# Layers of a transformer on one core: two hand-ordered stages get their orders from a search over priorities

## The chip, the cores and the metric

The kernel runs on one core of one Trainium2 chip. The metric is the device time of one launch in microseconds (us). A core has a matrix engine (PE, with its weight loads shown as PEld), a vector engine (DVE), an activation engine (ACT), a general engine (POOL) and a sync engine (SP) that issues most loads. Each engine takes its instructions in the order in which the program lists them, and waits for what the others have to deliver.

## The reference

The reference runs two layers of a first block on 256 latent and 256 context tokens of width 1024, and then one layer of a second block on the latent tokens. All is float32. Only the mixers of the first block's two layers matter here.

```python
# layer 0, half of the mixer: a delta rule over time, 8 heads of 64, forwards and backwards,
# first over the context, then over the latent tokens
def step(state, inp):
    r_t, w_t, k_t, v_t, kk_t, a_t = inp
    sa = jnp.einsum('bhvk,bhk->bhv', state, -kk_t)
    state = (state * w_t[:, :, None, :] + sa[..., None] * (kk_t * a_t)[:, :, None, :]
             + v_t[..., None] * k_t[:, :, None, :])
    return state, jnp.einsum('bhvk,bhk->bhv', state, r_t)
...
out_lat = jnp.concatenate([a_lat, b_lat], axis=-1) @ w_out
# layer 1's mixer: neighbourhood attention (8 heads) beside global attention (8 heads, 2 of keys),
# both with the context's keys and values, then w_out
```

After each mixer come a normalised residual, a squared-ReLU MLP (1024 to 4096 to 1024) and another residual.

## The kernel before, in words

Weights are split into a rounded part and a rest (`whi` on ACT, `wlo` on DVE, lines 608 and 609), activations likewise, and each product is made of three passes on PE. Loads of 512 KB (`raw`) come over SP's queue into a ring of three buffers.

Most of the kernel is put in order by the compiler's own scheduler. Two stages are not: between `flow.open` and `flow.close` every call on an engine is only recorded, with what it reads and writes, and `close` then issues all of them in an order of its own for PE, DVE, ACT and POOL. In the profile all of their instructions have line 501, where `close` issues them. SP's issues stay with the compiler's scheduler.

The first such stage is the delta rule. For each of 4 tiles (two heads each) `kappa(t)` normalises keys (with an rsqrt on POOL, `rsn`). For each of 16 blocks (tile, direction, context or latent) `rwkv_par` makes the decays (`sg`, `cs`, `E`, `kr`, `bk`), the masked products `GK`, `Gt`, then five rounds of a triangular inverse (`Tp` on DVE, `pq` on PE, `Qm` on DVE, `px` or `psT` on PE, `Sp` on ACT), and the matrices `KX`, `QM`. `rwkv_rec` carries the state over four chunks (`yp` on PE, `S` on DVE and ACT). `rwkv_out` normalises a finished tile (`yN`, `sqy`, `moA`). Beside these chains stand pieces that nothing in the stage waits for soon: 12 calls of `ada_chunk` (modulation weights of later stages, `psT<-raw,sT`, PE tiles of 128x32), three projections of the delta rule's own inputs for tile 3, and the first part of the output projection (`proj0`). PSUM banks are shared out in rings: banks 0 and 1 for the preparation, 2 for `pq`, 3, 4 and 5 one for each block in flight, 6 for the recurrence, 7 for `ada_chunk`, `gates_out` and `rwkv_out` in program order.

The second stage is layer 1's mixer: projections, rsqrts for the normalised heads (`rk`, `rq` on POOL), the bias sums `bC`, 8 calls of `attn4`, and the output projection.

The order comes from `order`. `links` finds for each recorded operation what it must wait for, and its `way`, the longest chain of durations from it to the end. `order` then plays the stage through: at each step, of the operations of the engine that can start first, those that could start within 100 ns of the earliest are compared, and the one with the longest way is taken. PE has a bonus of 2000 ns of way for staying in the same tile shape, and a price of 100 ns for changing it. The durations are formulas, for instance (line 343 for DVE, 347 for POOL; `both` is 2 in the delta rule, 1.05 in the mixer):

```python
o.dur = 150 + 2.8 * n if op.endswith("scan") else 150 + 1.03 * n if psum else 170 + (self.both if ins > 1 else ...) * n
...
o.dur = 1650 if k.get("op") == OP.pow else 200 + (1.3 if ... else 2.4 if self.both > 1.5 or op != "tensor_scalar" else 3.2) * n
```

The time at which the last engine is free in this play is the tally, `self.span`.

Of the kernel before, what the change touches and what calls it, by code (L numbers as in the profile page):

```python
# [3 lines left out]

# [262 lines left out]
class _Flow:  # L267
# [156 lines left out]
                p = ops[j]  # L424
                p.way = max(getattr(p, "way", 0), o.way + (p.tail if p.key != o.key else 0))

    def order(self, slack=100, stay=2000):
        self.links()
        ops = self.ops
        nxt, left = [[] for _ in ops], [len(o.pre) for o in ops]  # L430
        for i, o in enumerate(ops):
            o.new = [r for r in {x[0] for x in o.w + o.r if isinstance(x[0], _Root)} if r.place is None and r.heir is None]
            for j in o.pre:
                nxt[j].append(i)
        ready, free, mode, grid = {i for i, n in enumerate(left) if not n}, {}, None, {}
        idle, out = {}, []
        for r in self.roots:
            if r.place is None and r.heir is None:
                r.todo = len(r.ops)
                idle.update({x: 0 for x in r.places})  # L440
        while ready:
            start = {}
            for i in ready:
                o = ops[i]
                st = max(o.at, free.get(o.key, 0))
                if o.key == "T":
                    st = max([st] + [grid.get(c, 0) for c in o.parts[0][0]]) if o.mode == mode else \
                        max([st] + [x + 100 for x in grid.values()])
                for r in o.new:
                    if r.place is None:  # L450
                        st = max(st, min((idle[x] for x in r.places if x in idle), default=1e12))
                start[i] = st
            best = {}
            for i in ready:
                best[ops[i].key] = min(best.get(ops[i].key, 1e12), start[i])
            key = min(best, key=best.get)
            assert best[key] < 1e12
            i = max((i for i in ready if ops[i].key == key and start[i] <= best[key] + slack),
                    key=lambda i: (ops[i].way + (stay if key == "T" and ops[i].mode == mode else 0), -i))
            ready.discard(i)  # L460
            o, st = ops[i], start[i]
            for r in o.new:
                if r.place is None:
                    r.place = min((x for x in r.places if x in idle), key=lambda x: idle[x])
                    del idle[r.place]
            end = st + o.dur
            if o.key == "T":
                mode, at = o.mode, st
                for cells, n, recs in o.parts:

                    at = max([at] + [grid.get(c, 0) for c in cells])
                    for c in cells:
                        grid[c] = at + n
                    end = at + n
                    at += 7 * recs
                free["T"] = at
            else:
                free[o.key] = end
            out.append((st, i))
            for r in o.new:  # L480
                r.todo -= 1
                r.till = max(getattr(r, "till", 0), end + o.tail)
                if not r.todo:
                    idle[r.place] = r.till
            for j in nxt[i]:
                left[j] -= 1
                ops[j].at = max(ops[j].at, end + (o.tail if ops[j].key != o.key else 0))
                if not left[j]:
                    ready.add(j)
        self.span = max(free.values())  # L490
        return [i for _, i in sorted(out)]

    def close(self, engines):
        self.on = False
# [12 lines left out]
def body(ctx: ExitStack, tc: tile.TileContext, A, out, dbg=None):  # L507
# [982 lines left out]
    def proj_rows(W, x_of, tiles, done, order=(0, 1, 2, 3), between=None):  # L1490


        ps = {i: B_O0("pso") for i in tiles}
        for n_, q in enumerate(order):
            wh, wl = wchunk(W, q * 256, 2, 0, 512)
            for i in tiles:
                for k in range(2):
                    mmX(ps[i], *x_of(2 * q + k, i), wh[:, k, :], wl[:, k, :], n_ + k == 0, n_ == 3 and k == 1)
        if between is not None:
            between()  # L1500
        ws = wrows(W, 0, 8, 512)
        for i in tiles:
            p_ = B_O1("pso")
            for k in range(8):
                mmX(p_, *x_of(k, i), *ws[k], k == 0, k == 7)
            done(i, [ps[i], p_])
# [682 lines left out]
```

## Time and profile before

| | us |
|---|---|
| median of 3 runs | 1804.53 |
| lowest and highest | 1802.65, 1807.39 |
| the profiled execution | 1798.13 |
| its span, first to last instruction | 1796.2 |

The profile shows one execution. Busy times are those of an engine's instructions; a PE matmul's end is modelled. The granted clock is a mean over a stretch, 1.00 for TensorE's full speed. In lists of waits each line says which engine waited, for which engine's result, how long in total, how often, and the longest.

### The profile page before, as it was taken

Reading aid. Unit: us, or ns where it says so; the run is one execution under the profiler, and the core shown is the slowest. Engines: PE = TensorE matmul, PEld = TensorE weight load, DVE = VectorE, ACT = ScalarE, POOL = GpSimd, SP = SyncE. Lnnn points to the kernel's source line nnn. Section 1 sums busy time; section 2 is a strip of 40 time slices with the busy share of each in tenths; the row PEclk is TensorE's granted clock in tenths of the full one; section 3 lists DMA queues with packets and bytes.
Section 4 is the critical chain, followed back from the end, with each engine's and each line's share of the span. In section 5 each row is a group of like instructions: output and inputs, shape, how many; then the busy total and the mean of one; then the engine's idle time right before and its main releaser. Section 6 shows DMA issues by size and latency. Waiting matters only on the chain.

```text
span 1796.2 us, 33992 instructions
## 1 busy us (share of the span) xinstructions
PE 1715.3 (95%) x13601; PEld 1440.3 (80%) x13601; DVE 1082.0 (60%) x1965; ACT 884.1 (49%) x1703; POOL 447.2 (25%) x512
## 2 busy tenths in 40 slices
PE   6999899999898999999998999899989999999998
PEld 4777677767577888888887887799978889989997
DVE  3577577766656334444464775655566686568776
ACT  4555245544345554443443655545555554446553
POOL 1120344542413343333332213311120211110000
PEclk9999899999899999999998999999999999999999
DMA  9322141222264454444423322465547436655553
GB/s 311 108 59 60 37 140 51 96 74 95 72 198 142 131 169 147 141 141 141 141 82 87 89 71 71 132 197 187 188 152 226 129 93 174 190 156 187 177 183 121
DMA packets 185407, 240.08 MB, mean 134 GB/s; under 512 B 8961, under 2 KB 127889, under 8 KB 185121
## 3 DMA queue, kind: packets, MB, share of 16 engines
q1 hardware_dynamic: 183056, 229.68, 41.1%
q0 software_dynamic: 1904, 7.70, 1.3%
q8 instruction: 107, 1.75, 0.4%
q10 hardware_dynamic: 288, 0.52, 0.1%
q14 instruction: 52, 0.42, 0.1%
HBM read 236.83 MB, written 1.05 MB: 132 GB/s over the span
## 4 chain that ended last, share of the span: by engine, by line
PE 86%; DVE 5%; DMA 3%; ACT 2%; POOL 2%; issue 2%; SPq 0%; POOLq 0%; DVEq 0%; ACTq 0%
PE psT L623 9%; PE psT L625 9%; PE psT L624 9%; PE psT L501 9%; PE pf L628 6%; PE pf L629 6%; PE pf L630 6%; PE px L501 3%; PE ssp L501 2%; PE psr L501 2%; PE psU L623 2%; PE psU L625 2%; PE psU L624 2%; PE pq L501 2%; PE yp L501 2%; PE psS L501 2%
## 5 line engine op out<-in xcount | busy, mean ns | idle before, releaser
L609 DVE TENSOR_TENSOR wlo<-raw,whi 128x1024 fp32r<-128x1024 f32 x291 | 358.4, 1239 | 245.7 <-ACT whi L608 242.6
L608 ACT ACTIVATE whi<-raw 128x1024 fp32r<-128x1024 f32 x291 | 306.4, 1056 | 235.2 <-PE psT L624 121.6
L623 PE MATMUL psT<-uh,whi 128*128 128x256 f32 (+1 forms) x1032 | 332.4, 327 | 2.8 <-ACT uh L909 1.2
L624 PE MATMUL psT<-ul,whi 128*128 128x256 f32 (+1 forms) x1032 | 330.7, 321 | 0.0
L625 PE MATMUL psT<-uh,wlo 128*128 128x256 f32 (+1 forms) x1032 | 328.4, 321 | 0.0
L623 PEld LDWEIGHTS psT<-uh,whi 128*128 128x128 f32 x1032 | 193.3, 189 | 21.6 <-ACT uh L909 1.7
L624 PEld LDWEIGHTS psT<-ul,whi 128*128 128x128 f32 x1032 | 193.4, 188 | 17.9 <-issue 1.1
L625 PEld LDWEIGHTS psT<-uh,wlo 128*128 128x128 f32 x1032 | 193.5, 188 | 16.1 <-issue 0.3
L630 PE MATMUL pf<-whi,hlo 128*128 128x512 f32 x472 | 182.4, 390 | 0.0
L629 PE MATMUL pf<-wlo,hh 128*128 128x512 f32 x472 | 182.3, 390 | 0.0
L628 PE MATMUL pf<-whi,hh 128*128 128x512 f32 x472 | 181.9, 392 | 0.0
L1512 POOL TENSOR_TENSOR ffr<-ffr 128x512 f32<-128x512 f32 (+1 forms) x64 | 64.3, 1004 | 283.2 <-ACT hh L1511 251.7
L630 PEld LDWEIGHTS pf<-whi,hlo 128*128 128x128 f32 x472 | 88.6, 188 | 18.8 <-issue 0.2
L629 PEld LDWEIGHTS pf<-wlo,hh 128*128 128x128 f32 x472 | 88.6, 188 | 17.5
L628 PEld LDWEIGHTS pf<-whi,hh 128*128 128x128 f32 x472 | 88.5, 188 | 17.5
L623 PE MATMUL psU<-uh,whi 128*128 128x256 f32 x352 | 99.0, 282 | 1.0 <-DVE cv L2101 1.0
L624 PE MATMUL psU<-ul,whi 128*128 128x256 f32 x352 | 98.5, 280 | 0.0
L625 PE MATMUL psU<-uh,wlo 128*128 128x256 f32 x352 | 98.5, 280 | 0.0
L1513 DVE TENSOR_TENSOR hlo<-ffr,hh 128x512 fp32r<-128x512 f32 (+1 forms) x64 | 47.6, 743 | 76.9 <-POOL ffr L1512 76.9
L717 POOL TENSOR_TENSOR adac<-adac,wadc 128x512 f32<-128x512 f32 x56 | 76.2, 1361 | 64.0 <-ACT wadc L715 50.4
L715 ACT ACTIVATE wadc<-wadc,sT 128x512 f32<-128x512 f32 x56 | 40.5, 724 | 98.3 <-DMA wadc<-in_w_ada_dram 96.8
L623 PEld LDWEIGHTS psU<-uh,whi 128*128 128x128 f32 x352 | 66.6, 189 | 1.9 <-ACT whi L608 0.9
(775 smaller groups left out, 3603.1 us busy)
## 6 DMA issues: line engine op xcount, KB each, us to landing
raw<-in_w_ff_dram SPq DMA_DIRECT2D x128, 512.0 KB, 4.5
raw<-in_w_in_dram SPq DMA_DIRECT2D x50, 512.0 KB, 4.4
raw<-in_w_ada_dram SPq DMA_DIRECT2D x48, 512.0 KB, 4.7
raw<-in_w_ffn_up_dram SPq DMA_DIRECT2D x44, 512.0 KB, 4.8
wadc<-in_w_ada_dram SPq DMA_DIRECT2D x64, 256.0 KB, 2.9
raw<-in_w_out_dram SPq DMA_DIRECT2D x24, 512.0 KB, 3.7
raw<-in_w_ffn_down_dram SPq DMA_DIRECT2D x22, 512.0 KB, 4.5
raw<-in_w_in_even_dram SPq DMA_DIRECT2D x21, 512.0 KB, 4.2
```

The lines of the kernel that those rows point to most:

```text
L501: b = f(*map(real, a), **{n: real(x) for n, x in k.items()})
L608: S.activation(hi[:, :tot], raw[:, :tot], AF.Copy)
L609: V.tensor_tensor(lo[:, :tot], raw[:, :tot], R(hi[:, :tot]), op=OP.subtract)
L623: T.matmul(p_, wh, xh, start=first, stop=False)
L624: T.matmul(p_, wh, xl, start=False, stop=False)
L625: T.matmul(p_, wl, xh, start=False, stop=last)
L628: T.matmul(p_, xh, wh, start=first, stop=False)
L629: T.matmul(p_, xh, wl, start=False, stop=False)
L630: T.matmul(p_, xl, wh, start=False, stop=last)
L717: G.tensor_tensor(acc, acc, w, op=OP.add)
L1512: G.tensor_tensor(r_, r_, r_, op=OP.mult)
L1513: V.tensor_tensor(hl_, r_, R(hh), op=OP.subtract)
```

## The change

`order` now calls the old procedure, renamed `greedy`, once with the ways from `links`, and then 400 times with changed ways. For each trial it takes 1, 3 or 10 places in the list of operations, and adds to the ways of 1, 1, 5, 20 or 80 operations from there a number between -15000 and 15000 ns. A trial whose tally is not longer than the best so far becomes the base of the next. The best schedule's order, and its places for those PSUM tiles that have a choice, are issued. The random numbers are seeded, so the program is the same each time. `close` is as before, and so are the recorded operations, their durations and what they wait for.

```diff
-    def order(self, slack=100, stay=2000):
+    def order(self, rounds=400):
+
         self.links()
-        ops = self.ops
+        rng, way = random.Random(1), [o.way for o in self.ops]
+        best = self.greedy(way)
+        for _ in range(rounds):
+            w, n = list(way), len(way)
+            for _ in range(rng.choice((1, 3, 10))):
+                k, m, d = rng.randrange(n), rng.choice((1, 1, 5, 20, 80)), rng.uniform(-15e3, 15e3)
+                for x in range(k, min(n, k + m)):
+                    w[x] += d
+            new = self.greedy(w)
+            if new[0] <= best[0]:
+                best, way = new, w
+        self.span, seq, places = best
+        for r, x in places:
+            r.place = x
+        return seq
+
+    def greedy(self, way, slack=100, stay=2000):
+        ops, taken = self.ops, []
+        for r in self.roots:
+            if r.places is not None:
+                r.place, r.till = None, 0
+        for o, x in zip(ops, way):
+            o.way, o.at = x, 0
...
-        self.span = max(free.values())
-        return [i for _, i in sorted(out)]
+        return max(free.values()), [i for _, i in sorted(out)], taken
```

## Rows read from the trace of the kernel before

**Rows 1.** The page: PE's busy time; shares of the chain that ended last.

```profile
PE 1715.3 (95%) x13601; PEld 1440.3 (80%) x13601; DVE 1082.0 (60%) x1965; ACT 884.1 (49%) x1703; POOL 447.2 (25%) x512
...
PE 86%; DVE 5%; DMA 3%; ACT 2%; POOL 2%; issue 2%; SPq 0%; POOLq 0%; DVEq 0%; ACTq 0%
```

**Rows 2.** Windows: stretch: length, busy PE, PEld, DVE, ACT, POOL, granted clock, DMA share, GB/s.

```profile
182.00:531.00 349.00, 326.03 (x5022) 240.02 (x5019) 229.48 (x566) 157.37 (x418) 141.77 (x194) 0.95 0.29 92
531.00:550.00 19.00, 15.38 (x79) 11.95 (x77) 13.12 (x24) 11.54 (x27) 7.29 (x12) 0.95 0.66 231
950.00:1126.00 176.00, 170.22 (x1132) 143.56 (x1132) 108.83 (x201) 89.87 (x174) 44.09 (x42) 0.97 0.28 81
```

**Rows 3.** Waits of PE, 182 to 531 us: total, times, longest.

```profile
PE pq L501 <- DVE Qm L501: 2.8, 4, 0.9
PE psr L501 <- POOL rsn L501: 2.7, 1, 2.7
PE ssp L501 <- POOL kr L501: 2.4, 1, 2.4
...
PE ssp L501 <- DVE sq L501: 0.8, 1, 0.8
...
PE psT L501 <- DMA raw<-in_w_ada_dram: 0.4, 1, 0.4
...
PE pq L501 <- DVE adaT L501: 0.2, 1, 0.2
```

**Rows 4.** Windows of three parts of the delta rule's stretch.

```profile
182.00:450.00 268.00, 253.66 (x4145) 188.29 (x4143) 181.28 (x455) 123.50 (x340) 117.21 (x162) 0.97 0.26 83
450.00:490.00 40.00, 33.70 (x445) 23.06 (x434) 28.26 (x71) 16.55 (x46) 20.80 (x28) 0.79 0.25 80
490.00:531.00 41.00, 38.67 (x451) 28.66 (x447) 19.94 (x42) 17.32 (x33) 3.76 (x4) 1.00 0.52 164
```

**Rows 5.** Windows of the head of each stage.

```profile
190.00:210.00 20.00, 17.91 (x66) 11.67 (x67) 8.60 (x15) 3.78 (x8) 7.94 (x10) 0.74 0.18 53
960.00:1000.00 40.00, 35.75 (x227) 32.15 (x227) 18.28 (x31) 16.57 (x28) 7.82 (x9) 0.87 0.38 101
```

**Rows 6.** Timeline of PE, 448 to 477 us: start, length, what, idle before.

```profile
448.57 1.06 PE L501 MATMUL psT<-raw,sT 128*32 128x512 f32 x8
...
457.74 0.33 PE L501 MATMUL px<-Gt,Tp 64*64 64x128 f32 x2 [0.77 <-ACT RHS L501]
...
461.62 0.44 PE L501 MATMUL yp<-S,KX 128*64 128x128 f32 x4 [1.51 <-POOL KX L501]
...
468.69 1.22 PE L501 MATMUL psr<-lora,W 64*128 64x256 f32 x2 [1.11 <-ACT Gt L501]
...
472.56 1.22 PE L501 MATMUL ssp<-lora,A 64*128 64x256 f32 x2 [1.25 <-ACT RHS L501]
...
476.45 1.94 PE L501 MATMUL psT<-raw,sT 128*32 128x512 f32 x8 [0.52 <-DVE sqy L501]
```

**Rows 7.** Timeline of PE in the mixer.

```profile
974.01 0.60 PE L501 MATMUL prk<-cst_ci,rky 128*2 128x128 f32 x4 [3.96 <-POOL rky L501]
```

**Rows 8.** Timeline of POOL in the mixer.

```profile
969.80 2.11 POOL L501 TENSOR_TENSOR bC<-rpbT,cst_c 128x512 f32<-128x512 f32 x1 [6.57 <-DMA rpbT<-in_c_rpb_dram]
...
972.28 1.67 POOL L501 TENSOR_TENSOR rky<-rk,neghalf 128x8 f32<-128x8 f32 x1
```

**Rows 9.** Groups by form, 182 to 531 us: count, busy us, mean ns, idle before.

```profile
L501 DVE TENSOR_TENSOR Qm<-pq,cst_c 128x256 f32<-128x256 f32 x80 | 33.5, 419 | 19.6 <-PE pq L501 18.9
L501 DVE TENSOR_TENSOR wlo<-raw,whi 128x1024 fp32r<-128x1024 f32 x11 | 13.9, 1261 | 8.1 <-ACT whi L501 8.1
...
L501 POOL TENSOR_TENSOR kr<-kk,sg 128x256 f32<-128x256 f32 x16 | 13.2, 825 | 1.5 <-ACT sg L501 1.5
```

**Rows 10.** Instructions of the tile sg: ns min/median/max, first and last start.

```profile
L501 POOL TENSOR_TENSOR sg<-cs,sg x16: 718/728/1612, 197.5 to 473.3; 128x256 f32<-128x256 f32 x16
```

**Rows 11.** PE's group of ada_chunk's first products, 182 to 531 us.

```profile
L501 PE MATMUL psT<-raw,sT 128*32 128x512 f32 x192 | 27.3, 643 | 0.9 <-DVE sqy L501 0.5 <-DMA raw<-in_w_ada_dram 0.4
```

More of the change, by code (lines that the diff above doesn't have):

```diff
@@ L1 @@
 import math
+import random
 import re
@@ L464, in order @@
                     r.place = min((x for x in r.places if x in idle), key=lambda x: idle[x])
+                    taken.append((r, r.place))
                     del idle[r.place]
@@ L481, in order @@
                 r.todo -= 1
-                r.till = max(getattr(r, "till", 0), end + o.tail)
+                r.till = max(r.till, end + o.tail)
                 if not r.todo:
```

## The prediction

> **What bounds the kernel.** I read the page first: PE is busy 1715.3 of 1796.2 us, and PE holds 86% of the chain that ended last [rows 1]. So time can come only from PE's idle time, from stretches in which its clock is not granted in full, or from PE work that is removed. The change removes no instruction, so the third is out. Its reach is the two stretches whose order is written by `close`; the windows cut them out. The delta rule (with layer 0's first output projection) runs from 182 to 531 us: 349.0 us, PE busy 326.03. Layer 1's mixer runs from 950 to 1126 us: 176.0 us, PE busy 170.22 [rows 2]. What follows each on PE is issued by another scheduler, and the hole of 3.6 us in 531 to 550 [rows 2] is not the order's.
>
> Idle PE is therefore 349.0 - 326.03 = 23.0 us in the first and 176.0 - 170.22 = 5.8 us in the second. The waits view says how the 23 us are made up: 20 rows, the longest 2.8 us in four pieces (a masked product on DVE), then single waits of 2.7 and 2.4 us for POOL, down to 0.2 us [rows 3]. No single producer is late; many chains are a little late at different places. That is what an order can mend, and also what another order can bring back elsewhere.
>
> The clock is the second store. Granted clock was 0.97 in 182 to 450, 0.79 in 450 to 490 and 1.00 in 490 to 531 [rows 4]; the clock has two levels, 2.4 and 1.2 GHz. Time not granted: 268 x 0.03 + 40 x 0.21 = 8.0 + 8.4 = 16.4 us. Of this 20 x 0.26 = 5.2 us lie in 190 to 210, at the head of the stage [rows 5]. In the mixer 40 x 0.13 = 5.2 us lie in 960 to 1000 [rows 5], and 176 x 0.03 = 5.3 says that this is all of it.
>
> Two pockets matter most. From 457.74 to 476.45 us PE starts seven groups late: its chains of three blocks have run down together, one waits for POOL (1.51 us), one for ACT (1.11), one for ACT again (1.25). A filler (`ada_chunk`, the 128*32 products) ran at 448.57, the next only at 476.45, where it waited for DVE's `sqy`: fillers and the outputs of the last finished tile share bank 7 in program order, which the search may not change, but it may run `rwkv_out` or the fillers earlier [rows 6]. In the mixer the transposes of `rky` stood 3.96 us at the head of PE [rows 7], because POOL did the 2.11 us bias sum `bC` just before the rsqrt [rows 8]. Priority decides that order on POOL, so the search can turn it round. The tally prices both, but `bC` had itself waited for a load (6.57 us idle before it), and the time of a load is the part that an order sees worst.
>
> **The change, part by part.** (1) `order` makes 401 schedules in place of one; this runs when the program is built, so it costs the chip 0 us and no instruction. (2) The first schedule of the search is the old one, and a new one is taken only where its tally is not longer. The tally therefore cannot get worse; the chip's time can. (3) What moves: the order on PE, DVE, ACT and POOL inside both stretches. Counts and shapes stay, so PE's 326 + 170 us of busy time stay but for the clock and the drains between tile shapes. (4) Loads: SP's issues are not under `close`'s order; a `raw` load follows the release of its buffer, so it moves with the split that frees it. PE waited for a load only 0.4 us in the delta rule [rows 3], so I cost moved loads at nothing; without that cover each late 512 KB load costs what PE has left to do in front of it.
>
> How far does the tally see what the chip does? By its price formulas a masked product from PSUM is 150 + 1.03 x 256 = 414 ns, a POOL product 200 + 2.4 x 256 = 814 ns; the trace has 419 and 825 [rows 9]. These hold within 2%. But `wlo` is priced 170 + 2 x 1024 = 2218 ns and takes 1261 [rows 9], and the clock is not in the tally at all. So an order fitted to it keeps waits that it did not see.
>
> POOL's `sg<-cs,sg` took 728 ns in the median and 1612 ns at worst [rows 10], under one price of 814. The Trainium skill (SBUF — State Buffer, Summary: rules for kernel authors) says that when a DVE instruction has two SBUF inputs while a GpSimd one reads SBUF, whichever issues second waits until the first is done. By that rule the row's tail is a matter of order that no fixed price holds, and it speaks against trusting the tally: with the median price the sum below stands at -11 us, with two such waits more for each block at -3, the collision rival.
>
> The sum, each with both ends:
> - Delta rule, idle. Of 23.0 us the two waits of the head (2.7 for the rsqrt of the first `kappa`, 0.8 for its copy `sq`) [rows 3] hang on one chain with nothing in front, so 19.5 are in reach. Ends: 0 (nothing transfers) and -19.5. The prices that hold cover the chains DVE-PE-POOL, those that do not cover the weight splits, so I take a half found, and a third of that given back in waits that the tally does not see: 9.75 x 2/3 = -6.5.
> - Delta rule, clock. 16.4 - 5.2 (head) = 11.2 in reach; low clock follows idle PE in these rows (0.79 where 6.3 of 40 us are idle). Ends 0 and -11.2. In proportion to the idle time won, 6.5 / 19.5 x 11.2 = 3.7; some of it lay on idle time already, so -3.
> - Mixer. The 4.0 us wait is gone or stays; its 5.2 us of clock go with it in part. Ends 0 and -9. With PE 97% busy there is little else, and a load decides part of it: -1.5.
> - Behind the stages: the holes are those of other code; 0, ends -2 and +2.
> Sum: -6.5 - 3 - 1.5 = -11 us. The profiled execution took 1798.13 us (span 1796.2), the runs have a median of 1804.53, 0.36% above. The sum is made on the profiled one, 1798.1 - 11 = 1787.1; carried over to the median it is 1804.5 - 11 = 1793.5 us.
>
> **Rivals.**
> - *The tally improves, the chip does not* (0 us, 1804.5; -5 to +5). The waits move to places that the tally misprices. For it: 20 waits from 0.2 to 2.8 us, a `wlo` priced 1.8 times too long, no clock. Against it: the prices on the long chain hold within 2%. That the search finds nothing, which leaves the program as it was, belongs here too.
> - *DVE and POOL collide more often.* One collision cost 1612 - 728 = 0.88 us. Two more for each of 16 blocks are 28 us of POOL time; PE waited on POOL for 2.7 + 2.4 + 1.5 = 6.6 of 23 us [rows 3, 6], so I let 29% of it, 8 us, reach PE: -11 + 8 = -3, 1801.5. With one more for each block it would be 1797.5, still my forecast's side.
> - *Slower: the fillers are spent early.* The 12 `ada_chunk`s are 27.3 us of PE time in their first products [rows 11], 2.3 us each, which stand between the late chains of the last blocks. A tally that gains by running them sooner leaves 490 to 510 bare, as 456 to 476 is now. Priced by that stretch: idle 6.3 / 40 and clock 0.21, together 0.37 us for each us, over 20 us +7.4, with the gain elsewhere gone: 1811.9. It decides once the last filler runs before some 470 us. Against it: way lengths put fillers last, and changes are drawn for all operations alike.
> - *Much more is found*: all 19.5 us of idle in reach but the clock as it is, or the half with all its clock: about -20, 1784.5.
>
> **How the numbers follow.** Forecast -11 (own range 1787 to 1799) 0.44; the large gain 0.14; tally alone 0.20; collisions 0.07; fillers 0.15. A measurement of this kernel tells about 0.3%, 5.4 us, from no change. Faster by more than that: 0.44 + 0.14 = 0.58. Within: 0.20 + 0.07 = 0.27. Slower: 0.15. The range takes in the large gain and most of the filler case: 1783 to 1809 us, which leaves out the tops of both.
>
> **What would show it.** Right: PE's idle time in the first stretch falls from 23 to 16 or 17 us, granted clock in it rises from 0.95 towards 0.96, the pocket near 456 to 476 has a filler or a third chain in it, and the wait for `rky` is under 1 us. Both stretches keep their busy time to within some us. Wrong: idle time as before but in other places (tally alone); POOL's maxima above 1 us on more than a few products (collisions); the last 128*32 product before 470 us and a second low-clock stretch behind it (fillers); or all the difference lying outside 182 to 531 and 950 to 1126, where no order was changed.

## The result, and the profile after

The kernel after takes 1786.62 us in the median (1785.88 to 1787.69, 4 runs), the kernel before 1803.59 beside it (1800.10 to 1807.39, 4 runs): a ratio of 0.9898 [0.9879, 0.9918] (the record's estimate with its 95% interval; the quotient of the two medians is 0.9906), 17.0 us faster. The two profiled executions stand closer: 1798.13 and 1785.88 us, 12.2 apart. The profiled one of before was 5.5 us under the median of its runs, that of after 0.7 under; these some 4.7 us are the difference. They go with the clock: it was 0.976 in the profiled execution of before, while in 57 timed runs of that kernel in later sessions it went from 0.966 to 0.977 (medians 0.972 and 0.973) and the time from 1811.9 to 1796.5 us, the long times at the low clocks. What follows is read from the two traces, so it accounts for 12.1 us of span.

The page after: the span and PE's busy time. In this kernel `close` issues from line 525; the line numbers behind it have moved by 24 too.

```profile
span 1784.1 us, 33976 instructions
...
PE 1711.7 (96%) x13601; PEld 1437.2 (81%) x13601; DVE 1087.0 (61%) x1965; ACT 883.1 (50%) x1703; POOL 450.5 (25%) x512
```

The counts of instructions are those of [rows 1], so the difference is order alone. (The chain that ended last can be followed back only to 560.94 us here, so its shares are not set against those of [rows 1].) To find the place, the same instructions are looked up in both traces. From the delta rule's first `ssp<-cst_c,sq` (187.67 before, 186.94 after) to the last tile of its output, the last `moAl` (536.2 and 523.1), after is 12.4 us shorter. Up to the weight load of the last `psSh<-cst_ci,st_n` (929.8 and 916.4) 0.3 more is won, in layer 1's mixer up to `psSh<-cst_ci,st_n1f` (1133.2 and 1118.1) 1.7 more. Together with the 0.7 ahead of the first stage that is 15.1 us; behind the mixer 3.0 are given back, which leaves 12.1.

The windows of before between these landmarks (columns as in [rows 2]): the delta rule, the pocket of [rows 6], the mixer, and what follows it.

```profile
187.70:536.20 348.50, 325.53 (x5017) 239.76 (x5016) 230.96 (x566) 159.58 (x421) 142.51 (x195) 0.95 0.30 96
...
456.00:477.00 21.00, 15.01 (x148) 9.59 (x148) 16.10 (x37) 9.11 (x27) 14.99 (x20) 0.66 0.01 1
929.60:1133.20 203.60, 194.83 (x1261) 162.67 (x1259) 130.59 (x236) 108.10 (x214) 53.97 (x57) 0.97 0.27 81
1133.20:1156.00 22.80, 18.83 (x130) 17.05 (x129) 13.81 (x20) 11.96 (x27) 9.83 (x11) 0.85 0.26 86
```

The same four in the kernel after:

```profile
186.90:523.10 336.20, 320.03 (x5008) 236.06 (x5008) 228.97 (x566) 157.56 (x418) 144.10 (x195) 0.96 0.30 99
...
456.00:477.00 21.00, 17.86 (x206) 12.37 (x208) 13.79 (x38) 7.88 (x24) 10.30 (x15) 0.76 0.06 15
916.30:1118.10 201.80, 193.72 (x1260) 161.60 (x1258) 134.99 (x235) 107.97 (x214) 56.60 (x56) 0.97 0.26 80
...
1118.10:1141.00 22.90, 17.66 (x96) 15.70 (x95) 12.82 (x18) 9.63 (x22) 6.96 (x9) 0.70 0.19 63
```

In the delta rule, length less busy PE is the idle time: 23.0 us before, 16.2 after. The clock that was not granted is length times (1 - granted clock). Two digits over the whole stretch are too coarse for it, so it is summed over sixteen equal windows of the stretch: 17.2 us before, 11.8 after. What is left, 348.5 - 23.0 - 17.2 and 336.2 - 16.2 - 11.8, is 308.3 in both (idle time that lies in a stretch of low clock is counted in both stores, so this rest is arithmetic and not a measure of work). So the 12.3 us read as 6.8 of idle time and 5.4 of clock. The fall of the busy time, 325.53 to 320.03, fits that clock: the same matmuls at the higher level for longer. Behind the mixer the granted clock is 0.70 where it was 0.85: 6.9 and 3.4 us not granted, which covers the loss there. The changed order of the mixer did not make that loss. In the profiles of the fourteen kernels below, what follows the mixer took 665.0 to 666.7 us in twelve, eight of them with the mixer's old order; only before (663.0) and e12_neutral3 (662.7) were shorter.

PE's waits after, from 181.3 to 518 us, read beside [rows 3]:

```profile
PE pq L525 <- DVE Qm L525: 3.0, 4, 1.5
PE psr L525 <- POOL rsn L525: 2.7, 1, 2.7
PE yp L525 <- ACT S L525: 1.2, 2, 0.8
PE psT L525 <- DMA raw<-in_w_ada_dram: 1.1, 3, 0.5
PE ssp L525 <- POOL kr L525: 1.0, 1, 1.0
...
PE ssp L525 <- DVE ic L525: 0.3, 1, 0.3
```

There are 16 rows now for 20, down to 0.3 us. The two largest are as before: `Qm` four times, and the head's `rsn`, which has nothing to stand in front of it. The wait for `kr` fell from 2.4 to 1.0 us, that for loads rose from 0.4 to 1.1.

### The profile page after: what moved, and what is told of

Same layout as the page of the kernel before. It is cut to its first block, busy times and chain, and to the rows that moved or that the text cites. A ratio compares the mean times of both kernels' runs of the same rounds, so it can differ in the third digit from the quotient of the medians.

```text
span 1784.1 us, 33976 instructions
## 1 busy us (share of the span) xinstructions
PE 1711.7 (96%) x13601; PEld 1437.2 (81%) x13601; DVE 1087.0 (61%) x1965; ACT 883.1 (50%) x1703; POOL 450.5 (25%) x512
## 4 chain that ended last, share of the span: by engine, by line
PE 57%; DVE 3%; DMA 3%; ACT 2%; POOL 2%; issue 1%; POOLq 0%; SPq 0%; DVEq 0%; ACTq 0%
PE psT L647 7%; PE psT L649 7%; PE psT L648 7%; PE pf L652 5%; PE pf L653 5%; PE pf L654 5%; PE psT L525 5%; PE psU L647 2%; PE psU L649 2%; PE psU L648 2%; DMA wadc<-in_w_ada_dram 2%; PE psS L525 2%; PE pssk L525 1%; PE psN L823 1%; PE psO L525 1%
## 5 line engine op out<-in xcount | busy, mean ns | idle before, releaser
L648 PEld LDWEIGHTS psT<-ul,whi 128*128 128x128 f32 x1032 | 194.6, 189 | 18.4 <-issue 1.4
L649 PEld LDWEIGHTS psT<-uh,wlo 128*128 128x128 f32 x1032 | 194.4, 189 | 16.2 <-DVE wlo L633 0.4
```

Source lines behind the costliest of these rows:

```text
L648: T.matmul(p_, wh, xl, start=False, stop=False)
L649: T.matmul(p_, wl, xh, start=False, stop=last)
```

## The experiments

Each kernel below is the kernel before with one line changed: `close` takes a stored order, found ahead of time by a search over the same recorded operations, in place of the one that `order` makes. A stage without a stored order keeps the old one. Nothing is left out of the computation. The short diffs further down are of the search that made each list; the tallies are those of the play run over the stored lists.

```diff
-        seq = self.order()
+        seq = given(self)          # a stored list for 1813 operations (delta rule) or 631 (mixer)
...
+def given(flow):
+    seq = flow.order()
+    if len(flow.ops) in _ORD:
+        seq, places = _ORD[len(flow.ops)]
+        for r, x in places:
+            flow.roots[r].place = x
+    return seq
```

The theory on trial was that of the prediction: the shorter tally takes idle time out of the delta rule. Its main rival was that the tally says little, and that any other order would do. The medians, beside 1803.6 to 1805.6 for before in the same sessions, with the record's ratios; the last four columns are of the profiled execution, for the delta rule's stretch (each kernel's own landmarks):

| kernel | tally, delta rule | median us | ratio [95%] | length | idle PE | clock not granted | rest |
|---|---|---|---|---|---|---|---|
| before | 322.0 | 1804.5 | | 348.5 | 23.0 | 17.2 | 308.3 |
| after | 315.2 | 1786.6 | 0.9898 [0.9879, 0.9918] | 336.2 | 16.2 | 11.8 | 308.3 |
| e1_delta | 315.2 | 1789.2 | 0.9912 [0.9891, 0.9933] | 339.7 | 18.3 | 13.6 | 307.8 |
| e2_mixer | 322.0 | 1801.4 | 0.9984 [0.9968, 1.0] | 350.6 | 22.9 | 20.4 | 307.3 |
| e3_seed2 | 314.2 | 1791.9 | 0.9922 [0.9901, 0.9942] | 342.7 | 20.1 | 17.1 | 305.5 |
| e6_long | 313.4 | 1793.5 | 0.9936 [0.9923, 0.9949] | 339.4 | 21.3 | 13.6 | 304.5 |
| e5_neutral | 322.0 | 1791.1 | 0.9923 [0.991, 0.9937] | 340.5 | 22.7 | 10.2 | 307.5 |
| e9_neutral2 | 321.8 | 1799.0 | 0.997 [0.9955, 0.9985] | 343.9 | 21.7 | 13.8 | 308.5 |
| e12_neutral3 | 322.1 | 1791.2 | 0.993 [0.9913, 0.9947] | 343.2 | 21.1 | 13.7 | 308.4 |
| e4_worse | 329.5 | 1808.9 | 1.003 [1.0014, 1.0046] | 359.1 | 26.6 | 20.4 | 312.0 |
| e10_worse2 | 329.5 | 1807.9 | 1.002 [1.0007, 1.0032] | 353.9 | 23.6 | 22.1 | 308.2 |
| e7_price | 322.1; 311.4 by its own prices | 1789.4 | 0.9915 [0.9902, 0.9929] | 335.0 | 18.4 | 8.4 | 308.3 |
| e8_late | 315.2 | 1777.9 | 0.9848 [0.9831, 0.9864] | 336.9 | 16.9 | 11.8 | 308.3 |
| e11_both | as e7_price | 1781.0 | 0.9874 [0.9855, 0.9893] | 335.3 | 18.6 | 8.4 | 308.3 |

**One stage at a time.** e1_delta has the delta rule's order of the change and the old mixer, e2_mixer the reverse.

```diff
 _ORD = {
     1813: (...),        # e1_delta keeps this entry alone
-    631: (...),         # e2_mixer keeps this one alone
 }
```

> Only the delta rule takes the searched order (tally 322.0 to 315.2 us); layer 1's mixer keeps the old one. Theory (the gain is PE idle time and clock won in the delta rule): 11 to 17 us faster than the kernel before, PE idle in the stretch near 16 us, and nearly all of the whole change. Rival (the two stages share the gain, or it comes from what lies behind them): less than two thirds of the whole change, under 9 us.

> Only layer 1's mixer takes the searched order (tally 162.5 to 161.5 us); the delta rule keeps the old one. Theory (the mixer won 1.6 us and lost it again in the low clock behind it): within 3 us of the kernel before. Rival (the mixer carries a real part): 4 us or more faster. Its wait of some 4 us for the rsqrt rky should stand in both, since the tally does not see the load that makes it.

The delta rule alone gives 15.2 us (1804.5 - 1789.2), as the theory had it, though its idle PE was 18.3 us and not near 16. The mixer alone gives 3.1, with an interval that reaches 1.0; their sum is 18.3 and the change gave 17.0. In e2_mixer PE still waits 4.0 us for `rky`, so if the mixer gained anything, it was not where it was expected.

e1_delta runs the delta rule in the order of after, yet its stretch took 3.5 us more. The window from 380 to 420 us of e1_delta:

```profile
380.00:420.00 40.00, 36.57 (x642) 26.93 (x642) 26.66 (x66) 19.05 (x54) 22.82 (x30) 0.91 0.28 86
```

and that of after:

```profile
380.00:420.00 40.00, 38.66 (x702) 29.06 (x704) 28.79 (x75) 19.64 (x56) 22.83 (x30) 0.96 0.33 107
```

In this window PE of e1_delta waits for a load, as its timeline shows:

```profile
403.92 1.06 PE L501 MATMUL psT<-raw,sT 128*32 128x512 f32 x8 [1.48 <-DMA raw<-in_w_ada_dram]
```

So one order, executed twice, can differ by some 3 us. The mixer shows more: its old order, in ten of these profiles, took 200.4 to 206.9 us between the landmarks used above (before: 203.4). No profile of one execution tells orders apart that are closer than that.

**Other searches for a short tally.** e3_seed2 draws other changes, e6_long goes on for some 2500 trials.

```diff
-        rng, way = random.Random(1), [o.way for o in self.ops]      # 400 rounds
+        rng, way = random.Random(2), [o.way for o in self.ops]      # e3_seed2; e6_long: more rounds
```

> The delta rule takes another order, from the same search with another seed (tally 314.2 us, 7.9 below the old one and 1.0 below the first search's); the mixer keeps the old one. Theory (the chip follows the tally): 11 to 18 us faster than before, like the first seed. Rival (the first seed was lucky on the chip, the tally is blind to waits that matter): anywhere from no gain to 8 us.

> The delta rule takes the order after some 2500 trials of the same search (tally 313.4 us, 1.8 below that of 400); the mixer keeps the old order. Theory (the chip follows the tally): 1 to 5 us faster than the delta rule's order of 400 trials alone (1789.2 us). Rival (the last gains are fitted to the tally's own errors): the same or slower than that.

Both are faster than before, so the gain is not the luck of one seed. But both have a shorter tally than e1_delta and neither is faster than it: 1791.9 and 1793.5 against 1789.2, where e6_long was expected 1 to 5 us ahead. Below some 315 us the tally no longer says which order is better.

**Orders with the old tally, and with a worse one.** The same walk of 400 trials, with another rule for what it keeps.

```diff
-            if new[0] <= best[0]:
+            if abs(new[0] - first[0]) < 500:                  # e5_neutral, e9_neutral2, e12_neutral3 (ns)
+            if best[0] <= new[0] <= limit:                    # e4_worse, e10_worse2: about 2.3% above the old
                 best, way = new, w
```

> The delta rule takes an order that a walk of 400 changes reached while its tally was held within 0.5 us of the old one (322.0 us); the mixer keeps the old order. Theory (the chip follows the tally): within 5 us of the kernel before. Rival (the old order held a pocket by chance, and nearly any reshuffle removes it): 8 us or more faster, at an unchanged tally.

> A second walk of 400 changes with the delta rule's tally held within 0.5 us of the old one, other seed; the mixer keeps the old order. Theory now (the old order was a slow one among those of its tally, by where its idle time lay for the clock): 7 us or more faster than before again. Rival (the first walk was lucky, the tally does rank orders): within 5 us of the kernel before.

> A third walk at the old tally, third seed, mixer old. Same theories: 7 us or more faster if the old order was an outlier; within 5 us if the first walk was lucky. If one of the two is fast and the other not, orders of one tally spread by some 15 us, and the searched gain cannot be put down to the tally alone.

> The delta rule takes an order found by the same changes of priorities, but walked the other way, to a tally of 329.5 us, 7.5 above the old one; the mixer keeps the old order. Theory (the chip follows the tally, with the clock on top): 7 to 17 us slower than before. Rival (any other order than the old one is as good, the old one held a bad pocket by chance): no slower, or faster.

> A second walk up to a tally of 329.5 us for the delta rule, other seed; the mixer old. If the tally ranks orders over a distance of 15 us: 15 us or more slower than the searched ones (1804 us or more, as the first such walk with 1808.9). If it ranks nothing: as the others, near 1791 us.

Here the theory loses its simple form. Three orders with no better tally than the old one are faster by 14.6, 5.5 and 13.3 us. (e9_neutral2 falls between its two forecasts, 7 or more and up to 5.) The old order is thus a slow one among orders of its own tally, and three walks out of three that only left it gained. Yet the tally is not blind: the two orders at 329.5 are slower than before by 4.4 and 3.4 us, under the 7 to 17 expected of the first, and slower than all the others. The searched orders lie ahead of those at 322 by little: the best of the three, e5_neutral, has an interval that takes in the ratios of e1_delta and e3_seed2. e5_neutral shows what a tally can't hold. The window of its delta rule:

```profile
187.00:527.50 340.50, 317.76 (x4994) 233.90 (x4993) 225.01 (x565) 156.19 (x416) 140.48 (x195) 0.97 0.30 96
```

Idle PE is 340.5 - 317.76 = 22.7 us, as before. The stretch is 8.0 us shorter all the same, and 7.0 of these are clock: 10.2 us not granted for 17.2. For e4_worse, the other way:

```profile
186.50:545.60 359.10, 332.46 (x5019) 243.60 (x5018) 229.90 (x567) 160.65 (x423) 142.52 (x197) 0.94 0.29 94
```

26.6 us idle, 20.4 not granted. Less these two stores the stretch is 304.5 to 312.0 us in all fourteen kernels; the stores together run from 26.8 us (e7_price) to 47.0 (e4_worse).

One execution says little of the clock, but the record lists the granted clock of every timed run. So the split can be made over the whole kernel and all runs: not granted is a run's span times (1 - granted clock), the rest is its time less that. Medians; the clock is listed to 0.001, which is 1.8 us.

| kernels | tally, delta rule | not granted, us | rest of the time, us |
|---|---|---|---|
| before, three sessions | 322.0 | 48.7 to 50.5 | 1753.4 to 1755.5 |
| e5_neutral, e9_neutral2, e12_neutral3 | 321.8 to 322.1 | 34.0, 42.2, 36.7 | 1755.9, 1754.4, 1754.2 |
| e2_mixer, e7_price | 322.0, 322.1 | 48.6, 37.5 | 1752.1, 1751.9 |
| after, e1_delta, e3_seed2, e6_long | 315.2 to 313.4 | 38.4, 40.2, 44.8, 44.8 | 1748.2, 1748.4, 1747.0, 1748.1 |
| e4_worse, e10_worse2 | 329.5 | 48.8, 51.5 | 1759.2, 1756.7 |

So the tally does rank what it holds: the rest is 1747.0 to 1748.4 us at 315 and below, 1751.9 to 1755.9 at 322, and 1756.7 to 1759.2 at 329.5. It does not rank the clock, and what the three walks won is clock alone. Of the change's 17.0 us some 5 to 7 are rest and 10 to 12 clock. Why one order is granted more clock than another is not shown.

**Prices put right.** DVE's price of an instruction with two SBUF inputs, which the prediction found 1.8 times too long for `wlo`, is set by the trace, and the search run again.

```diff
+            if abs(o.dur - (170 + 2 * n)) < 2:
+                if n >= 512: o.dur = 170 + 1.08 * n
+                elif nm == "b_": o.dur = 170 + 1.2 * n
```

> The delta rule's order comes from 400 trials with DVE's prices set to what the trace has: 170 + 1.08 n for sums of two SBUF operands of 512 columns and more (the weight split from 2218 to 1276 ns, measured 1261), 170 + 1.2 n for the product b_ (measured some 475 ns); the mixer keeps the old order. Theory (the wrong price of the split keeps waits): 3 us or more faster than the delta rule's order of 400 trials alone (1789.2 us). Rival (DVE has slack, its price hardly matters): within 3 us of it.

1789.4 against e1_delta's 1789.2: no gain in the whole, where 3 us or more were expected, though its stretch is the shortest of all (335.0 us, 8.4 of clock not granted). The run does not show that right prices are worth nothing to a search: played by e7_price's prices, e1_delta's order has a tally of 310.3, shorter than the 311.4 that this search reached, and by the old prices e7_price's order stands at 322.1, as before does. What can be said is that the wrong prices do not explain why before is slow. By the right ones before has 318.4, the three walks 316.3 to 317.7, the orders of after, e3_seed2 and e6_long 308.4 to 311.0, and the two worse ones 324.5 and 325.9: the same groups.

**The load in front of `bC`.** In the play, `bC` can start as soon as the mixer opens, because the load of `rpbT` is not among the recorded operations. e8_late says in the play that it comes 30 us in. The delta rule has the order of after; the mixer's tally stays at 161.5. The two lists of the mixer give every engine the same order but for one instruction: the first `bC` stands third on POOL, behind `rk` and `rky`, in place of first.

```diff
-            o.way, o.at = x, 0
+            o.way, o.at = x, getattr(o, "late", 0)     # 30000 for the operations that write bC
```

> The searched orders of both stages as in the changed kernel, but in the mixer's play the bias sums bC may not start before 30 us, which puts the first of them behind the rsqrt rky on POOL (the tally stays at 161.5 us). Theory (POOL's queue holds the rsqrt behind a sum that waits for a load, and the tally is blind to it): PE's wait of 3.7 us for rky is gone and the low clock behind it with it, 4 to 8 us faster than the changed kernel (1786.6 us). Rival (something else is late next, or the sum is then missing): within 2 us of it.

First POOL in the mixer of after (start, length, what, idle before):

```profile
956.03 1.19 POOL L525 TENSOR_TENSOR bC<-rpbT,cst_c 128x512 f32<-128x512 f32 x1 [6.51 <-DMA rpbT<-in_c_rpb_dram]
957.31 1.06 POOL L525 TENSOR_SCALAR rk<-ssk 128x8 f32<-128x8 f32 x1
958.45 1.67 POOL L525 TENSOR_TENSOR rky<-rk,neghalf 128x8 f32<-128x8 f32 x1
```

and PE of after, behind it:

```profile
960.18 1.01 PE L525 MATMUL prk<-cst_ci,rky 128*2 128x128 f32 x4 [3.74 <-POOL rky L525]
```

`bC` stands at the head of POOL for 6.51 us until its load lands, and `rk` and `rky`, which need no load, stand behind it. Then POOL in e8_late:

```profile
955.58 0.20 POOL L501 TENSOR_SCALAR rk<-ssk 128x8 f32<-128x8 f32 x1 [4.36 <-DVE ssk L501]
955.87 1.67 POOL L501 TENSOR_TENSOR rky<-rk,neghalf 128x8 f32<-128x8 f32 x1
957.72 1.20 POOL L501 TENSOR_TENSOR bC<-rpbT,cst_c 128x512 f32<-128x512 f32 x1 [0.18 <-DMA rpbT<-in_c_rpb_dram]
```

`rky` now goes first, and PE's wait for it is no longer among its waits from 936 to 1111 us:

```profile
PE psN L795 <- DVE ul L666: 0.9, 2, 0.7
PE pssk L501 <- DVE sqd L501: 0.6, 1, 0.6
```

Of e8_late, the windows of the mixer and of what follows it:

```profile
917.20:1112.40 195.20, 190.83 (x1260) 159.92 (x1258) 133.92 (x235) 108.13 (x214) 56.40 (x56) 0.99 0.28 82
1112.40:1135.00 22.60, 17.80 (x92) 15.48 (x91) 12.51 (x18) 9.17 (x22) 6.97 (x9) 0.62 0.21 64
```

The mixer is 6.6 us shorter than in after (201.8): idle PE 4.4 for 8.1, and granted clock 0.99 for 0.97, about 2.0 us not granted for 6.1. The idle time is the wait that is gone; the clock alone would not show it, since the old order's ten profiles had 2.0 to 10.4 us not granted in the mixer, but none of the ten had less than 8.8 us idle or took less than 200 us. At 1777.9 us e8_late beats both kernels, after by 8.7 us in the medians (4 to 8 were expected) and by 5.0 in the profiled executions. By the split over all runs, 32.8 us not granted and a rest of 1745.6, the 8.7 are some 3 of rest and 6 of clock.

**Both repairs.** e11_both has e7_price's delta rule and e8_late's mixer.

> The delta rule's order from the search with corrected DVE prices, and the mixer's order with the bias sums behind the rsqrt. If the two gains add: 1775 to 1780 us, faster than both kernels. If the corrected prices bring nothing on the chip: the same as with the first search's order beside that mixer, 1778 us.

1781.0 us, a little over both forecasts: it keeps the mixer's gain (194.6 us for that stretch) and adds none; e8_late stays the fastest.

## Why the prediction was right, point by point

- **The whole.** Forecast 1793.5, own range 1787 to 1799; measured 1786.6, 0.4 us under that range and inside the wide one. The sum for the profiled execution, -11, met -12.2. The carrying over to the median assumed that both profiled runs stand alike to theirs, and they did not (5.5 and 0.7 us under), which is the larger part of the miss. That -11 met -12.2 is luck in part: as the points below show, the clock's term was too small, the mixer's is not shown, and what lies behind went the other way.
- **Delta rule, idle: -6.5 forecast, -6.8 measured.** 23.0 fell to 16.2, inside the 16 to 17 foretold. The size is right, with luck: the two factors in it (a half found, a third given back) stand on no row, and the same order left 18.3 us in e1_delta and 16.9 in e8_late. That a shorter tally takes out this part is borne out, since the rest of the time follows the tally over all runs; but e5_neutral's gain has no idle time in it, and three of three walks at the old tally gained too.
- **Delta rule, clock: -3 forecast, -5.4 measured.** This is the term that was mis-sized. The profiles leave it wide (the old order had 20.4 us in e2_mixer, the new one 13.6 in e1_delta and 11.8 in e8_late, so 3.6 to 8.6); over all runs and the whole kernel it is 10 to 12. It was priced in proportion to idle time. In e5_neutral 7.0 us of clock came back with 0.3 us of idle time, so that proportion does not hold; that it hangs on where the idle time lies is a guess that no run here tests. The pocket is one place where both fell: from 456 to 477 PE had 6.0 us idle at 0.66 before, and 3.1 us idle at 0.76 after. The window is one of time and not of work: the last `ssp<-lora,A`, which came 1.25 us late at 472.56 [rows 6], starts at 457.53 in after without a wait.
- **The pocket's filler.** An `ada_chunk` came at 472.54 in after, 3.9 us earlier than before (476.45), and PE's gaps in front of it are 0.4 to 1.0 us, where they were up to 1.5. In part as foretold: the chains run down less deeply, and the filler comes at the end of the pocket, not in it.
- **Mixer: -1.5 forecast, -1.7 read off, and no gain shown.** The searched order took 201.7 us, and 200.9 in e2_mixer, between the same landmarks where ten profiles of the old order took 200.4 to 206.9; in e1_delta the old order took 202.1, 1.3 less than in before. So the near hit is luck. The sign foretold, a wait for `rky` under 1 us, did not come: 3.74 us in after for 3.96 [rows 7]. The prediction had said that the load in front of `bC` [rows 8] is what an order sees worst, and still took a part of the gain for won. The play takes that load to be there from the start, so it saw nothing to turn. e8_late shows that the place of this one instruction was worth four times the term (6.6 us of the stretch).
- **Behind the stages: 0 with ends of 2, measured +3.0.** Outside the ends. PE's hole behind the mixer was longer (5.2 us idle for 4.0 in the windows), and the clock stood lower there. As the fourteen profiles show, before is the exception here and not after, and eight kernels with the old mixer lost the same; what decides it is open.
- **The tally alone (0.20): refuted as a whole, right as a warning.** In the rest of its time the chip did follow from 329.5 down to 315. It did not below that, and three orders of one tally, 322, lay 8 us apart and up to 14.6 from the old one. The price of `wlo` does not account for that; the clock, which the tally does not hold, does (34.0 to 42.2 us not granted for some 50, at the same rest).
- **Collisions (0.07): not seen.** The median of POOL's `sg<-cs,sg` rose from 728 to 778 ns, that of `kr<-kk,sg` fell from 816 to 731, and the longest `sg` stayed at 1612; it is the first of the sixteen in both orders (197.45 and 197.05 us), so the new order did not move it. All of POOL's work in the stretch rose by 1.6 us (142.5 to 144.1), where the rival had 28. By the rule of the Trainium skill (SBUF — State Buffer, Summary: rules for kernel authors) a DVE instruction with two SBUF inputs and a GpSimd one that reads SBUF do not run side by side: the second to issue waits until the first is done. Such a tail would fit it, but no run here isolates it.
- **Fillers early (0.15): refuted.** The instructions of `ada_chunk`'s first products in after, nanoseconds min, median, max, first and last start:

```profile
L525 PE MATMUL psT<-raw,sT x192: 592/617/1061, 217.8 to 494.2; 128*32 128x512 f32 x192
```

The last start is 494.2 (500.2 before), 29 us ahead of the stage's end in place of 36, and far behind the 470 from which this rival decides. The clock from 490 to 531 is not lower than in [rows 4].

Which single move of the delta rule's new order mends most is open: the orders differ in many places at once, and no run undid one of them. Nor is it shown why the old order is slow among those of its tally. Its two stores, 40.2 us against 32.9 to 35.5 in the three walks, say in what it shows, not which choice makes it so.

## What to carry to other kernels

A tally that prices instructions well is a coarse sieve: here 15 us of it told fast orders from slow ones, and its last 2 us told nothing, so time several orders of near-equal tally and keep the fastest. Time some orders of the old tally as well: without these three the whole gain would have been put down to the tally, and more than half of it was clock, which orders with the old tally won too. Before searching longer or mending prices, put into the play what it does not hold: an operation that waits for a load outside the recorded stage stands at the head of an in-order engine and holds all behind it, and one earliest start for `bC` gave 8.7 us at an unchanged tally. Read idle time and clock not granted together, because an order can win by the second with the first unchanged.

## What the runs showed of the hardware

The clock that is not granted is a store as large as the idle time, and it can move alone: in e5_neutral 7.0 us of it came back with 0.3 of idle time. For the same instructions in a stretch of 335 to 359 us it was 8.4 us (e7_price) to 22.1 (e10_worse2), with idle PE between 16.2 and 26.6. What follows the mixer ran at one of three values in all fourteen profiles: 0.85 in before and e12_neutral3, 0.70 in after and six others, 0.62 to 0.63 in e8_late and four others; that is 3.4, 6.9 and some 8.5 us not granted in nearly the same 23 us. It does not go by how busy PE was ahead of it. The mixer and what follows it, first in e3_seed2 and then in e5_neutral, both with the mixer's old order:

```profile
918.70:1124.70 206.00, 197.20 (x1261) 164.65 (x1258) 130.00 (x237) 108.12 (x214) 54.11 (x57) 0.96 0.27 80
1124.70:1147.50 22.80, 17.97 (x94) 15.63 (x93) 12.80 (x17) 9.51 (x22) 8.28 (x9) 0.63 0.16 48
...
922.10:1122.70 200.60, 191.77 (x1260) 160.24 (x1258) 130.08 (x237) 108.24 (x214) 54.54 (x57) 0.99 0.28 82
1122.70:1145.50 22.80, 17.88 (x94) 15.64 (x93) 12.73 (x17) 9.41 (x22) 7.81 (x9) 0.63 0.15 47
```

One order of one stage, with 8.8 us idle both times, was granted 0.96 and 0.99, and the low clock behind it is the same.
